# A second of seven block products made from halved blocks, with VectorE's order written out

## Chip, cores and metric

One core of one Trainium2 chip. The metric is the time on the device, in microseconds, of one execution of the whole program. Engines: TensorE (PE) multiplies; VectorE (DVE) and ScalarE (ACT) work elementwise; GpSimd (POOL) is nearly idle; SyncE (SP) issues most DMA transfers in the order of its queue.

## The reference

A decoder block on x of 1024 rows and 1024 columns, in float32: a pooling mixer beside windowed attention, merged by gates, and then an MLP with normalisation around it. The change concerns the MLP's second multiplication and what feeds it:

```python
D_MODEL = 1024; SEQ = 1024; D_FF = 4 * D_MODEL
...
    h2 = _rmsnorm(x, g_mlp_pre[l])
    ff = jnp.einsum('bsf,fd->bsd',
                    jnp.square(jax.nn.relu(jnp.einsum('bsd,df->bsf', h2, w_up[l]))), w_down[l])
    x = x + _rmsnorm(ff, g_mlp_post[l])
```

Below f is the squared relu (1024 x 4096), w_dn is w_down (4096 x 1024), and Down is f times w_dn with the closing normalisation.

## The kernel before

Every large matmul is made on operands split into a high and a low part: `split(hi, lo, src)` casts `src` to `hi` on ScalarE (L101) and subtracts to get `lo` on VectorE (L104). Each product then takes three matmuls, high by high, high by low, low by high (`PASSES`). The tiles of split parts are called `wh` for f and `ar` for w_dn; `raw` and `st` are staging tiles of unsplit data, `B` are resident tiles of w_dn's four blocks (B11, B12, B21, B22).

Down is computed as 2 x 2 blocks by a scheme with seven block products instead of eight. The sums of f that the scheme needs are made in the up stage (`store()`, called for pairs of row tiles) and kept in DRAM (`f_dram`, seven column blocks, `A_OF` tells which one a product reads). The sums and differences of w_dn's blocks are made in Down on VectorE (`differences`, `last_weights`, and the line in `operands` for product 5). `PRODUCTS = (1, 5, 2, 3, 6, 7, 4)` is the order of the products. Each has 8 steps over the contraction (`s_`), so Down has 56 steps, numbered j. In a plain step `down_mm` (L2075) makes 24 matmuls of 128x128 by 128x512 into four PSUM banks.

Product 6 is made by the same scheme once more, on blocks halved again: `quarters` prepares a step and `quarters_mm` (L2055) makes 42 matmuls with 256 columns in it, seven parts of six. Such a step needs four split operands: f1 (the block's own quarters), f2 (three sums of quarters of f, kept in DRAM in `spill`), w1 (three quarters of the weight block), w2 (four sums T of quarters of the weight block, L2009 to L2011). Three of the seven parts are added onto what product 1 left in `u` (`ONTO`, copied into the banks by ScalarE at L2050). `quarters_close` (L2061 to L2069) adds the seven parts up into `u` at the end.

While TensorE works on step j, the operands of step j + 2 are prepared (`AHEAD`). The scheduler of the language orders each engine's instructions, except inside `manual_schedule`, where the order of the code is kept: before, VectorE's order is given for the operands of products 6, 7 and 4, and the last step of product 6. An engine takes its instructions in that order and waits at each for what it needs. Tiles come from pools with a fixed number of buffers, and a new tile's first writer waits for the last reader of the buffer's old one. So f2 and w2 of a halved step s + 2 wait for the end of TensorE's step s, and w1 of step s + 1 waits for the sixth part of step s.

Names of weights: `wh<-raw` with 768 elements is f2's low part, `ar<-T` with 1024 is w2's, `ar<-B` with 512 and 256 is w1's (two pieces), `wh<-raw` with 1024 is f1's or that of a plain step's f.

Of the kernel before, what the change touches and what calls it, by code (L numbers as in the profile page):

```python
# [8 lines left out]
F32 = mybir.dt.float32  # L9
# [5 lines left out]
P = 128  # L15
# [35 lines left out]
def block_kernel(ctx: ExitStack, tc, xt, x, consts, vecs, sinks, b_qkv, g_post, g_mlp, g_mlp_post,  # L51
# [1565 lines left out]
    def up_close0(m, f):  # L1617
# [4 lines left out]
        def store():  # L1622
# [11 lines left out]
            if m // 2 % 2 == 0:  # L1634
                dve.tensor_tensor(s2[:, 256:], s2[:, :256], s2[:, 256:], ALU.subtract)
                s2_even.append(s2)
            else:
                a = s2_even.pop()
                e = g32([3, 256])
                dve.tensor_tensor(e[:, 1, :], s2[:, 256:], a[:, 256:], ALU.subtract)  # L1640
                dve.tensor_tensor(e[:, 0, :], e[:, 1, :], a[:, :256], ALU.add)
                dve.tensor_tensor(e[:, 2, :], s2[:, :256], e[:, 1, :], ALU.subtract)
                q.dma_start(e_dram(m // 4), e)
# [5 lines left out]
    stores, s2_even = [], []  # L1649

    def e_dram(s_):
        return spill[s_][:, :768].rearrange("p (a b) -> p a b", b=256)
# [9 lines left out]
    def up_square(m, f):  # L1662
        act.activation(f, f, AF.Square)
        f_odd[m] = f
        nc.scalar.dma_start(f_dram[m // 2][:, 2:4, :], f.rearrange("p (a b) -> p a b", b=512))
# [271 lines left out]
    def acc4(name):  # L1937
        return [dl.tile([P, 512], F32, tag="acc", name=nm(name), bufs=12) for _ in range(4)]
# [11 lines left out]

    def resident(name, s_):
        t = rp.tile([P, 2, 512], F32, tag="w", name=nm(name))
# [3 lines left out]
    def streamed(name, s_):  # L1956
        t = raw_tile()
        nc.sync.dma_start(t, w_block(name, s_))
        return t

    behind = []

    def operands(i, s_):
# [3 lines left out]
        else:  # L1967
            ft = stage([2, 512]) if (i, s_) == (1, 3) else raw_tile()
            nc.sync.dma_start(ft, f_block(A_OF[i], s_))
            if i == 1:  # L1970
# [3 lines left out]
                wt = res["B11", s_]  # L1974
            elif i == 5:
                resident("B12", s_)
                wt = res["B11", s_]
                dve.tensor_tensor(wt, res["B12", s_], wt, ALU.subtract)
            elif i == 2:
                wt = streamed("B21", s_)  # L1980
            elif i == 3:
                resident("B22", s_)
                wt = res["B22", s_]
            elif i == 6:
                wt = res["B11", s_]
            elif i == 7:
                wt = res["B12", s_]
            else:
                wt = res["B21", s_]
        if i == 6:  # L1990
            quarters(s_, ft, wt)
            return
# [348 lines left out]
```

## Time and profile before

| What | Value |
| --- | --- |
| median of 3 runs | 1090.21 us (1090.16 to 1090.69) |
| the profiled execution | 1091.0 us |
| its span, first to last instruction | 1089.2 us, granted clock 0.999 |
| Down, from product 1's first matmul to the end | from 779.30 us |
| order of products in it | 1, 5, 2, 3, 6, 7, 4 |
| VectorE busy in all | 849.2 us (78%) |
| ScalarE busy in all | 625.5 us (57%) |

A row of groups reads: line, engine, operation, out<-in by the program's names, shapes, count, then busy us in all, mean ns of one, idle time of the engine ahead of them with its releaser. A row of waits reads: engine and line, the releaser, then us in all, times, and the longest. A row of the chain reads: start, us, engine, line, count. A row of the timeline reads: start, us, engine, line, operation, count, and in brackets the idle time before. In a timeline several instructions of one kind in a row stand together, with their time from the first start to the last end.

### The profile page before, as it was taken

What the parts mean: (1) busy time and instruction counts of PE and PEld (TensorE: products, weight loads), DVE (VectorE), ACT (ScalarE), POOL (GpSimd) and SP (SyncE); (2) the same over time, 40 slices, a digit from 0 to 9 for tenths busy, and PEclk for the clock granted to TensorE, in tenths of its full rate; (3) what the DMA queues carried; (4) which work ended last, traced back from release to release, by engine and by line L of the source; (5) the groups of instructions that cost most, each with busy time, mean ns of one, the idle gap of its engine ahead of it and who ended that gap; (6) DMA issues with size and microseconds to landing.
All of it is one profiled execution on the core that took longest, in us unless ns stands there. A gap on an engine that the chain in (4) does not pass through costs nothing.

```text
span 1089.2 us, 14332 instructions
## 1 busy us (share of the span) xinstructions
PE 1079.7 (99%) x5211; PEld 903.5 (83%) x5211; DVE 849.2 (78%) x1194; ACT 625.5 (57%) x1029; POOL 86.2 (8%) x142
## 2 busy tenths in 40 slices
PE   9999999999999999999999999999999999999997
PEld 8888888888888888888888888888888888898885
DVE  6688888989897887889876766665657867579996
ACT  7567886456654257567665554555446535476543
POOL 0354411100100012100000000000000000000000
PEclk9999999999999999999999999999999999999999
DMA  9666889679965776832566534445597873379622
GB/s 333 201 174 175 214 251 350 184 233 315 268 213 171 223 191 137 288 117 77 185 227 227 205 143 174 160 150 216 177 391 272 299 265 118 101 234 318 218 78 78
DMA packets 100921, 227.36 MB, mean 209 GB/s; under 512 B 10481, under 2 KB 28017, under 8 KB 100849
## 3 DMA queue, kind: packets, MB, share of 16 engines
q1 hardware_dynamic: 84416, 189.46, 50.8%
q0 software_dynamic: 10528, 16.78, 8.8%
q10 hardware_dynamic: 5904, 20.19, 4.8%
q8 instruction: 41, 0.67, 0.3%
q14 instruction: 32, 0.25, 0.1%
HBM read 161.38 MB, written 63.97 MB: 207 GB/s over the span
## 4 chain that ended last, share of the span: by engine, by line
PE 75%; DVE 4%; ACT 1%; issue 1%; DMA 1%; ACTq 0%; DVEq 0%
PE mm L583 18%; PE at L583 15%; PE at L2075 12%; PE mm L2075 11%; PE mm L1523 5%; PE mm L494 3%; PE at L2055 2%; PE at L1523 2%; PE at L1251 2%; PE mm L2055 2%; PE mm L1251 1%; PE mm L496 1%; PE at L1569 1%; DMA st<-in_w_g_dram 1%; DVE xf L2121 0%
## 5 line engine op out<-in xcount | busy, mean ns | idle before, releaser
L2075 PE MATMUL at<-ar,wh 128*128 128x512 f32 x552 | 126.0, 389 | 0.2 <-DVE ar L104 0.2
L2075 PEld LDWEIGHTS at<-ar,wh 128*128 128x128 f32 x552 | 103.4, 188 | 22.1 <-DVE ar L104 0.6
L2075 PE MATMUL mm<-ar,wh 128*128 128x512 f32 x528 | 120.5, 389 | 0.0
L2075 PEld LDWEIGHTS mm<-ar,wh 128*128 128x128 f32 x528 | 99.1, 188 | 20.5
L101 ACT CAST wh<-raw 128x1024 fp32r<-128x1024 f32 (+1 forms) x58 | 59.2, 1023 | 86.2 <-PE at L2075 37.0
L104 DVE TENSOR_TENSOR wh<-st,wh 128x512 fp32r<-128x512 f32 (+1 forms) x103 | 74.4, 733 | 38.9 <-ACT wh L101 34.3
L104 DVE TENSOR_TENSOR wh<-raw,wh 128x1024 fp32r<-128x1024 f32 (+1 forms) x58 | 68.4, 1186 | 40.8 <-ACT wh L101 40.6
L583 PE MATMUL mm<-T,wx 128*128 128x512 f32 x375 | 90.3, 389 | 0.0
L583 PEld LDWEIGHTS mm<-T,wx 128*128 128x128 f32 x375 | 70.4, 188 | 14.6
L583 PE MATMUL mm<-gr,wh 128*128 128x512 f32 x321 | 77.2, 391 | 0.0
L101 ACT CAST wh<-st 128x512 fp32r<-128x512 f32 (+2 forms) x102 | 65.8, 654 | 19.2 <-PE at L583 4.6
L583 PEld LDWEIGHTS mm<-gr,wh 128*128 128x128 f32 x321 | 59.9, 188 | 12.2
L583 PE MATMUL mm<-T,wh 128*128 128x512 f32 x267 | 66.0, 389 | 0.0
L104 DVE TENSOR_TENSOR ar<-B,ar 128x1024 fp32r<-128x1024 f32 (+2 forms) x51 | 50.9, 1011 | 14.7 <-ACT ar L101 14.4
L583 PE MATMUL at<-gr,wh 128*128 128x512 f32 x243 | 59.0, 389 | 0.0
L583 PE MATMUL mm<-x,wh 128*128 128x512 f32 x240 | 58.9, 394 | 0.0
L583 PEld LDWEIGHTS mm<-T,wh 128*128 128x128 f32 x267 | 50.1, 188 | 10.4
L101 ACT CAST ar<-B 128x1024 fp32r<-128x1024 f32 (+2 forms) x51 | 44.1, 882 | 19.3 <-PE mm L2055 6.4
L583 PEld LDWEIGHTS at<-gr,wh 128*128 128x128 f32 x243 | 45.6, 188 | 9.5
L583 PEld LDWEIGHTS mm<-x,wh 128*128 128x128 f32 x240 | 44.2, 188 | 9.6 <-ACT f L692 0.2
L583 PE MATMUL at<-T,wx 128*128 128x512 f32 x213 | 52.0, 389 | 0.0
L583 PEld LDWEIGHTS at<-T,wx 128*128 128x128 f32 x213 | 40.0, 188 | 8.3
(529 smaller groups left out, 2264.5 us busy)
## 6 DMA issues: line engine op xcount, KB each, us to landing
raw<-f_dram SPq DMA_DIRECT2D x52, 512.0 KB, 4.7
B<-in_w_dn_dram SPq DMA_DIRECT2D x32, 512.0 KB, 6.5
f_dram<-g SPq DMA_DIRECT2D x28, 512.0 KB, 2.8
st<-in_w_up_dram SPq DMA_DIRECT2D x24, 512.0 KB, 4.5
g<-spill_dram SPq DMA_DIRECT2D x17, 512.0 KB, 5.7
f_dram<-g ACTq DMA_DIRECT2D x17, 512.0 KB, 2.9
st<-in_w_g_dram SPq DMA_DIRECT2D x16, 512.0 KB, 4.7
g<-in_w_up_dram SPq DMA_DIRECT2D x15, 512.0 KB, 4.8
```

Of the source, the lines that this page charges most:

```text
L101: act.copy(hi, src)
L104: return eng.tensor_tensor(lo, src, f32(hi), ALU.subtract)
L494: pe.matmul(bs[th], whi[:, k, :], rhs(k, hl, th), start=k == 0 and hl == 0, stop=False)
L496: pe.matmul(bs[th], wlo[:, k, :], rhs(k, 0, th), start=False, stop=k == nk - 1)
L583: pe.matmul(b, w[wh][:, kt, :], x_, start=not after and kt == 0 and j == 0, stop=kt == 3 and j == 2, skip_group_check=after)
L1251: pe.matmul(b, w[wh][:, kt, :], xo[xh][:, kt, :], start=not after and kt == 0 and j == 0, stop=kt == 1 and j == 2, skip_group_check=after)
L1523: pe.matmul(bs[t], Am[a][k][ah][:, t * P:(t + 1) * P], Wm[w][k][wh], start=not after and k == 0 and j == 0, stop=k == 3 and j == 2, skip_g ...
L1569: pe.transpose(b[:, i, :], hs[4 * th + i][:, k * P:(k + 1) * P], ident)
L2055: pe.matmul(part[q][:, t, :], o[fs][fh][:, fk, t * P:(t + 1) * P], o[ws][wh][:, wk, :], start=q not in ONTO and (s_, t, j) == (0, 0, 0), s ...
L2075: pe.matmul(bs[t], fo[fh][:, k2, t * P:(t + 1) * P], wo_[wh][:, k2, :], start=not after and s2 == 0 and k2 == 0 and j == 0, stop=(s2, k2) ...
```

## The change

Product 2 is made as product 6 is, by seven products of halved blocks, and comes right behind product 1; the order becomes 1, 2, 5, 3, 6, 7, 4. Product 2's close writes to a new tile `c4` (it becomes `c11`), product 6's to `u4` as before. In the up stage `store()` also makes the quartered sums of f's column block 2, and half of one block is stored later. All of Down's VectorE order is the order of the code now: per step j first `operands(j + 2)`, then what `extras(j)` lists. Resident tiles of w_dn are queued on SP behind the f load of the step (`later`). The pool of resident tiles, the accumulators and the tags of PSUM banks are counted anew.

```diff
@@ up stage, store() @@
             if m // 2 % 2 == 0:
                 dve.tensor_tensor(s2[:, 256:], s2[:, :256], s2[:, 256:], ALU.subtract)
-                s2_even.append(s2)
+                dve.tensor_tensor(g[:, 256:512], g[:, :256], g[:, 256:512], ALU.subtract)
+                q.dma_start(fd[:, 2, :], g[:, :512])
+                evens.extend((g[:, :512], s2))
             else:
-                a = s2_even.pop()
-                e = g32([3, 256])
...
-                q.dma_start(e_dram(m // 4), e)
+                for i, b in ((2, g[:, :512]), (6, s2)):
+                    a = evens.pop(0)
+                    e = g32([3, 256])
+                    dve.tensor_tensor(e[:, 1, :], b[:, 256:], a[:, 256:], ALU.subtract)
+                    dve.tensor_tensor(e[:, 0, :], e[:, 1, :], a[:, :256], ALU.add)
+                    dve.tensor_tensor(e[:, 2, :], b[:, :256], e[:, 1, :], ALU.subtract)
+                    q.dma_start(e_dram(i, m // 4), e)
...
     def up_square(m, f):
...
-        nc.scalar.dma_start(f_dram[m // 2][:, 2:4, :], f.rearrange("p (a b) -> p a b", b=512))
+        j = 2 if m // 2 % 2 else 3
+        nc.scalar.dma_start(f_dram[m // 2][:, j:4, :], f.rearrange("p (a b) -> p a b", b=512)[:, j - 2:, :])
@@ Down @@
+    def later(name, s_):
+        with tc.issue_after(behind[0].ins):
+            resident(name, s_)
...
-        if i == 6:
-            quarters(s_, ft, wt)
+        if i in HALVED:
+            quarters(i, s_, ft, wt)
...
-    def differences(s_):
-        b11, b12, b22 = (res[n, s_] for n in ("B11", "B12", "B22"))
-        dve.tensor_tensor(b11, b22, b11, ALU.subtract)
-        w = halved(b11)
-        dve.tensor_tensor(b12, b22, b12, ALU.subtract)
-        tt = res["T", s_] = rp.tile([P, 4, 256], F32, tag="w", name=nm("T"))
+    def first_sum(s_):
+        dve.tensor_tensor(res["B11", s_], res["B12", s_], res["B11", s_], ALU.subtract)
+
+    def next_sums(s_):
+        for n in ("B11", "B12"):
+            dve.tensor_tensor(res[n, s_], res["B22", s_], res[n, s_], ALU.subtract)
+
+    def last_sum(s_):
+        dve.tensor_tensor(res["B11", s_], res["B21", s_], res["B11", s_], ALU.subtract)
+
+    def quarter_sums(name, s_):
+        w = halved(res[name, s_])
+        tt = res["T", s_] = rp.tile([P, 4, 256], F32, tag="T", name=nm("T"), bufs=4)
         dve.tensor_tensor(tt[:, 0:2, :], w[:, 1::2, :], w[:, 0:2, :], ALU.subtract)
         dve.tensor_tensor(tt[:, 2, :], w[:, 3, :], tt[:, 0, :], ALU.subtract)
         dve.tensor_tensor(tt[:, 3, :], w[:, 2, :], tt[:, 2, :], ALU.subtract)
...
-    PRODUCTS = (1, 5, 2, 3, 6, 7, 4)
+    PRODUCTS = (1, 2, 5, 3, 6, 7, 4)
+    HALVED = (2, 6)
...
+    def extras(j):
+        def at(first):
+            return 0 <= j - first < NS
+        if at(3):
+            later("B21", j - 3)
+        if at(4):
+            quarter_sums("B21", j - 4)
+        if at(11):
+            later("B12", j - 11)
+        if at(12):
+            first_sum(j - 12)
+        if at(16):
+            square_x1(j - 16)
+        if at(18):
+            later("B22", j - 18)
+        if 17 <= j < 21:
+            fin_half(j - 17, 0, c11[j - 17])
+        if at(20):
+            next_sums(j - 20)
+        if at(26):
+            quarter_sums("B11", j - 26)
...
+    def down_step(j, i, s_):
+        last = s_ == NS - 1
+        if i in HALVED and last:
+            with tc.manual_schedule(engines=CORE):
+                quarters_mm(i, s_)
+                quarters_close(c4 if i == 2 else u4)
+        if j + AHEAD < len(steps):
+            operands(*steps[j + AHEAD])
+        if i in HALVED:
+            if not last:
+                quarters_mm(i, s_)
+            extras(j)
+            return
...
+    with tc.manual_schedule(engines={mybir.EngineType.DVE}):
+        for j in range(1, AHEAD):
+            operands(*steps[j])
+        for j, step in enumerate(steps):
+            down_step(j, *step)
```

Two places on VectorE show the order. The first is the run of instructions for a halved step. Before, in product 6 (f2's low part, w2's, w1's in two pieces, f1's, and then the next step's f2, w2, w1 and f1):

```order
L104 TENSOR_TENSOR wh_8494<-raw_8491,wh_8493 128x768
L104 TENSOR_TENSOR ar_8496<-T_8219,ar_8495 128x1024
L104 TENSOR_TENSOR ar_8502<-B_1091_7123,ar_8501 128x512
L104 TENSOR_TENSOR ar_8502<-B_1091_7123,ar_8501 128x256
L104 TENSOR_TENSOR wh_8504<-raw_8489,wh_8503 128x1024
L104 TENSOR_TENSOR wh_8561<-raw_8558,wh_8560 128x768
L104 TENSOR_TENSOR ar_8563<-T_8225,ar_8562 128x1024
```

The same run after, in product 2 (L2007 to L2009 are the sums T that a later step uses):

```order
L104 TENSOR_TENSOR wh_7451<-raw_7448,wh_7450 128x768
L104 TENSOR_TENSOR ar_7453<-T_7386,ar_7452 128x1024
L104 TENSOR_TENSOR ar_7459<-B_1123_7332,ar_7458 128x512
L104 TENSOR_TENSOR ar_7459<-B_1123_7332,ar_7458 128x256
L104 TENSOR_TENSOR wh_7461<-raw_7446,wh_7460 128x1024
L2007 TENSOR_TENSOR T_7522<-B_1147_7436 128x512
L2008 TENSOR_TENSOR T_7522<-B_1147_7436,T_7522 128x256
L2009 TENSOR_TENSOR T_7522<-B_1147_7436,T_7522 128x256
L104 TENSOR_TENSOR wh_7531<-raw_7528,wh_7530 128x768
L104 TENSOR_TENSOR ar_7533<-T_7438,ar_7532 128x1024
```

Between f1 of one step and f2 of the next now stand the three instructions that make T. The second place is the close of a halved product. Before, at the end of product 6 (the operands of product 7's first step, the close, the operands of its second step):

```order
L104 TENSOR_TENSOR wh_8760<-raw_8757,wh_8759 128x1024
L104 TENSOR_TENSOR ar_8762<-B_1117_7271,ar_8761 128x1024
L2062 TENSOR_TENSOR st_8854<-st_8854,at_8369 128x512
L2063 TENSOR_TENSOR st_8855<-st_8854,at_8368 128x512
L2065 TENSOR_TENSOR u_7026<-u_7026,at_8368 128x2x256
L2066 TENSOR_TENSOR st_8855<-st_8854,at_8371 128x512
L2068 TENSOR_TENSOR u_7026<-st_8855,mm_8372 128x2x256
L2068 TENSOR_TENSOR u_7026<-st_8854,mm_8374 128x2x256
L2068 TENSOR_TENSOR u_7026<-st_8855,mm_8376 128x2x256
L2069 TENSOR_TENSOR u_7026<-u_7026,st_8855 128x2x256
L104 TENSOR_TENSOR wh_8871<-raw_8868,wh_8870 128x1024
L104 TENSOR_TENSOR ar_8873<-B_1123_7308,ar_8872 128x1024
```

After, at the end of product 2 (L1995 is `first_sum`, L2057 to L2064 the close, and the operands are those of product 5):

```order
L104 TENSOR_TENSOR wh_7873<-raw_7870,wh_7872 128x1024
L104 TENSOR_TENSOR ar_7875<-B_1089_7142,ar_7874 128x1024
L1995 TENSOR_TENSOR B_1103_7218<-B_1225_7867,B_1103_7218 128x1024
L2057 TENSOR_TENSOR st_7969<-st_7969,mm_7469 128x512
L2058 TENSOR_TENSOR st_7970<-st_7969,mm_7468 128x512
L2060 TENSOR_TENSOR c_7083<-u_7082,mm_7468 128x2x256
L2061 TENSOR_TENSOR st_7970<-st_7969,mm_7471 128x512
L2063 TENSOR_TENSOR c_7083<-st_7970,at_7472 128x2x256
L2063 TENSOR_TENSOR c_7083<-st_7969,at_7474 128x2x256
L2063 TENSOR_TENSOR c_7083<-st_7970,at_7476 128x2x256
L2064 TENSOR_TENSOR c_7083<-c_7083,st_7970 128x2x256
L104 TENSOR_TENSOR wh_7984<-raw_7981,wh_7983 128x1024
```

The close stands between the same two pairs of operands; differences for product 5 (`first_sum`) now stand in the same queue, one right ahead of the close, and others behind each further pair of operands.

163 lines of the change are left out of this document (54 added, 109 removed).

## The prediction

> **What bounds the kernel now.** I read the page's busy times first, then TensorE's waits, the end of the chain of waits, busy time by stage for the seven Down products, and the groups and timelines around product 6, which is already made as seven halved products and so is the model for product 2.
>
> ```profile
> span 1089.2 us, 14332 instructions
> PE 1079.7 (99%) x5211; PEld 903.5 (83%) x5211; DVE 849.2 (78%) x1194; ACT 625.5 (57%) x1029; POOL 86.2 (8%) x142
> PE mm L200 <- PEq L2327: 0.8, 1, 0.8
> PE sc L182 <- ACT x L203: 0.6, 1, 0.6
> PE at L2075 <- DVE ar L104: 0.2, 1, 0.2
> PE at L583 <- DVE z L1168: 0.2, 1, 0.2
> 779.30 43.52 PE at L2075 x192
> 822.82 43.52 PE mm L2075 x192
> 866.34 43.52 PE at L2075 x192
> 909.86 43.52 PE mm L2075 x192
> 953.38 2.87 PE at L2055 x24
> ```
>
> TensorE is busy for 99% of the span, and all its waits together are 1.8 us: matmuls bound the kernel. A plain product is 192 matmuls in 43.52 us (226.7 ns each, 5.44 us for a step of 24), without a gap. Product 2 is the third of them (866.34).
>
> ```profile
> 993.69 6.58 PE L2075 MATMUL at<-ar,wh 128*128 128x512 f32 x28
> 1000.47 7.78 PE L2075 MATMUL at<-ar,wh 128*128 128x512 f32 x33 [0.21 <-DVE ar L104]
> 779.30:822.80 43.50, 43.50 (x194) 36.03 (x193) 26.93 (x27) 19.37 (x22) 0.00 (x0) 1.00 0.87 317
> 953.40:993.70 40.30, 40.30 (x337) 40.19 (x337) 32.36 (x38) 31.44 (x44) 0.00 (x0) 1.00 0.79 255
> 958.26:988.50 30.24, 30.24 (x253) 30.13 (x252) 25.20 (x30) 22.17 (x31) 0.00 (x0) 1.00 0.83 269
> ```
>
> The last three rows are stretches: length, then busy time of TensorE, weight loads, VectorE, ScalarE and GpSimd, granted clock, DMA share, GB/s. Product 6 (halved) runs from 953.38 to 993.69: 336 matmuls of 256 columns in 40.31 us, 120 ns each, 5.04 us for a step of 42. The third stretch is six of its steps: VectorE is busy 25.20/6 = 4.20 of every 5.04 us. So 0.84 us per step is free on VectorE, and that is the number on which this change turns.
>
> **The change, part by part.**
>
> *Fewer matmul columns.* Product 2 goes from 43.52 to 40.32 us of TensorE: -3.2. [...]
>
> *VectorE's work per step.* A halved step needs the 4.20 us above, and its weight sums T on top. In before these sums lie ahead of product 6, where there is room; after, T for step s of product 2 is made four iterations of the step loop ahead of its use, so four of eight fall into product 2, and a fifth between the operands of its first and second steps. VectorE's order is now given, so nothing overtakes them.
>
> ```profile
> L2009 DVE TENSOR_TENSOR T<-B 128x512 f32<-128x512 f32 x8 | 5.5, 690 | 0.2
> L2011 DVE TENSOR_TENSOR T<-B,T 128x256 f32<-128x256 f32 x8 | 3.4, 424 | 0.2
> L2010 DVE TENSOR_TENSOR T<-B,T 128x256 f32<-128x256 f32 x8 | 3.4, 422 | 0.2
> 958.50 1.03 DVE L104 TENSOR_TENSOR ar<-B,ar 128x512 fp32r<-128x512 f32 x2 [1.96 <-ACT ar L101]
> 959.44 2.09 DVE L104 TENSOR_TENSOR wh<-raw,wh 128x1024 fp32r<-128x1024 f32 x2
> ACT ar L101 <- PE mm L2055: 6.4, 7, 1.3
> ```
>
> The sums cost 0.690 + 0.424 + 0.422 = 1.54 us, so a round with them is 4.20 + 1.54 = 5.74 us, 0.70 longer than TensorE's step. A lead cannot pay for that: the last row shows that ScalarE's first weight cast of the next step waits for TensorE to leave the tile, in each of seven steps, so VectorE is never more than about a step ahead.
>
> The start: in before VectorE begins the second step's first-half weights at 958.50, 5.12 us after product 6 began, behind ScalarE's copies. Into product 2 ScalarE has two more copies to make there, against a cast that can start earlier:
>
> ```profile
> 952.53 1.07 ACT L2251 COPY c<-mm 128x512 f32<-128x512 f32 x2
> 953.49 0.85 ACT L101 CAST wh<-raw 128x768 fp32r<-128x768 f32 x1
> 957.85 0.92 ACT L101 CAST ar<-B 128x512 fp32r<-128x512 f32 x2
> ```
>
> 5.12 + 1.07 - 0.3 (my estimate of the earlier cast) = 5.9 us after product 1's end, which is the clock's zero below.
>
> *The lateness at product 2's end.* VectorE, back to back:
>
> ```profile
> 993.15 0.68 DVE L2062 TENSOR_TENSOR st<-st,at 128x512 f32<-128x512 f32 x1
> ...
> 998.06 1.22 DVE L104 TENSOR_TENSOR wh<-raw,wh 128x1024 fp32r<-128x1024 f32 x1
> 999.20 1.22 DVE L104 TENSOR_TENSOR ar<-B,ar 128x1024 fp32r<-128x1024 f32 x1
> 1000.34 1.22 DVE L104 TENSOR_TENSOR wh<-raw,wh 128x1024 fp32r<-128x1024 f32 x1
> L1978 DVE TENSOR_TENSOR B<-B,B 128x1024 f32<-128x1024 f32 x8 | 9.8, 1220 | 0.9 <-DMA B<-in_w_dn_dram 0.9
> ```
>
> The close of a halved product takes 998.06 - 993.15 = 4.91 us, each 128x1024 operation 1.14 us start to start, a plain step's pair 2.28 us, and a difference for product 5 (the L1978 row, same form) 1.14 too. Five rounds with T: 5.9 + 28.7 = 34.6. One with a difference instead: 4.20 + 1.14, to 39.9. The last halved step's second half 2.1, to 42.0; difference 1.14; operands of product 5's first step 2.28, to 45.4; difference 1.14, to 46.6; close 4.91, to 51.5; operands of product 5's second step 2.36 (until the last one ends), to 53.8. TensorE then has 20 of that step's 24 matmuls left (four need only high parts; the 28 before the wait at 1000.47 are 24 + 4 of the same kind): 20 x 0.2267 = 4.53, to 58.4. Without waits these ten steps take 40.32 + 10.88 = 51.2. So 7.2 us late; 6.4 if VectorE starts at 5.12 as in product 6. As a floor I take 5.3: the list from 5.9 to 53.8 is 47.9 us long, and 4% off every operation (my estimate of how far such rows can be off) is 1.9.
>
> *Product 6.* Its T sums move too: five of eight lie in product 3, three between its own steps. Start at 5.12, three rounds of 5.74, to 22.3; TensorE has 35 of the fifth step's 42 matmuls left, 4.2, to 26.5 against 25.2 without waits: +1.3. The later rounds of 4.20 fit, so it stays at that. Low end 0, if high-part matmuls pulled ahead cover it.
>
> *Edits that I cost at nothing.* The up stage's extra halves: per pair one or three 128x256 subtractions and 384 KB of spill on every second pair. Four pairs with 0.42 and four with 1.26 us (L2011's row, 0.424) are 6.7 us of VectorE over some 330 us, in which TensorE waits for VectorE 0.2 us in all (the z row above). If the cover is gone it is at the entry to Down:
>
> ```profile
> 796.99 1.23 DVE L104 TENSOR_TENSOR wh<-raw,wh 128x1024 fp32r<-128x1024 f32 x1 [4.21 <-ACT wh L101]
> 798.67 1.23 DVE L104 TENSOR_TENSOR ar<-B,ar 128x1024 fp32r<-128x1024 f32 x1 [0.46 <-ACT ar L101]
> 806.91 1.22 DVE L104 TENSOR_TENSOR ar<-B,ar 128x1024 fp32r<-128x1024 f32 x1 [0.16 <-ACT ar L101]
> 809.57 1.23 DVE L104 TENSOR_TENSOR ar<-B,ar 128x1024 fp32r<-128x1024 f32 x1
> 790.00:795.00 5.00, 5.00 (x23) 4.13 (x22) 1.23 (x1) 1.05 (x1) 0.00 (x0) 1.00 1.03 397
> ```
>
> The fifth step's operands are done at 799.9; TensorE wants them at 779.30 + 21.76 = 801.1. 1.2 us are spare, and the DMA engines are full there (share 1.03 at 397 GB/s): 384 KB more are 1.0 us at that rate. I take 0, with +1 as the other end. The resident loads of B21 now stand in SP's queue behind each step's f, ahead of the next one: at 397 GB/s each pushes the later ones by 1.3 us, one ahead of the seventh step and two ahead of the eighth, which have 811.9 - 808.1 = 3.8 and 817.4 - 810.8 = 6.6 us to spare. In product 2 a step moves 512 + 384 + 512 KB in 5.04 us, 286 GB/s, below the 317 of product 1's row. Cost 0. Plain differences, squares of x1 and gains ride on VectorE's 16.6 idle us of a plain product (43.50 - 26.93). Accumulator buffers, tags and banks cost nothing by themselves: close reads a bank before TensorE's order comes to it, as in 6 to 7 now. Products 7 and 4 keep their content.
>
> **Sum.** -3.2 + 7.2 + 1.3 = +5.3 us. The profiled run took 1091.0 us (span 1089.2), 0.8 above the median of 1090.21; so 1096.3 for such a run, and 1095.5 by the median. A change of under 0.2% (2.2 us) could not be told from none here.
>
> **Rivals.**
> 1. *VectorE's lead absorbs the sums: faster, 1087.0.* Mechanism: high-part matmuls pulled ahead, together with the free 0.84 us, cover 1.54. For it: TensorE has no wait in product 6 today. Against it: 0.70 us per round in five rounds plus a close that lies ahead of operands. It decides where a round of VectorE with T is at most 5.04 us; the rows give 5.74. If the close's lateness alone stayed at 6 to 7's size (44.20 against 43.50 now, 0.7), the time is 1087.7. Chance 0.10.
>
> ```profile
> 993.70:1037.90 44.20, 43.99 (x195) 36.01 (x194) 42.89 (x57) 23.40 (x31) 0.00 (x0) 1.00 0.73 252
> ```
>
> 2. *The floor: stalls about as large as the saving.* 5.3 late at product 2, nothing in product 6: -3.2 + 5.3 = +2.1, 1092.3, or within 0.2%. Chance 0.13.
> 3. *Transfers late as well.* A halved step's spill load waits for a staging tile that VectorE's now late operands free, and ScalarE then waits for the spill:
>
> ```profile
> ACT wh L101 <- DMA raw<-spill_dram: 1.5, 2, 0.8
> ```
>
> 0.75 us each time; in five steps +3.7, over the sum: 1099.2. Against it: today only two of eight steps wait, and off the path. Chance 0.12.
> 4. *The forecast*, 1093 to 1098: 0.65.
>
> Slower holds 0.65 + 0.12 and a little of the floor, 0.78; same 0.12; faster 0.10. The range leaves out rival 1 and the upper part of rival 3: 1091 to 1099.
>
> **What would show it.** Right: in the changed kernel TensorE waits at the quartered matmuls for VectorE's ar and wh, some 0.7 us per step from product 2's third step on; one wait of about 3 us at product 5's second step, behind the close; product 2 lasting about 44.9 us (42.0 and its last 24 matmuls) in spite of 40.3 of work; VectorE busy for 98% from 6 us into product 2 to the close; about 1.3 us of waits in product 6's first half and none in its second. Wrong: no waits in product 2, or a VectorE that idles on ScalarE there (then a round is shorter than my sum, or the lead longer); waits on DMA at product 1's fifth step; product 6 longer than 42 us.

## The result, and the profile after

The changed kernel takes 1100.34 us (median of four, 1099.06 to 1101.33) against 1090.45 us (1090.16 to 1090.69) beside it: ratio 1.009, 95% interval 1.0073 to 1.0108. It is 9.9 us slower. The forecast was slower by 5.3, with a range that ended at 1099. The profiled execution is the shortest of the four, 1099.06 us; its span is 8.1 us longer than the one profiled before.

Busy times from the page, and TensorE's waits, of the changed kernel:

```profile
span 1097.3 us, 14810 instructions
PE 1080.7 (98%) x5355; PEld 907.8 (83%) x5355; DVE 888.0 (81%) x1282; ACT 638.6 (58%) x1053; POOL 86.4 (8%) x142
PE at L2070 <- DVE ar L104: 2.6, 2, 2.1
PE mm L2050 <- DVE ar L104: 2.0, 6, 0.6
PE at L2050 <- DVE ar L104: 0.3, 1, 0.3
```

TensorE now waits for VectorE at the halved matmuls (L2050), where it did not wait before, and at plain ones (L2070): 2.1 us at product 5's second step and 0.5 us at product 1's fifth. The waits listed are not all of the lateness: single matmuls that start late one by one are not in them. So I measured each stage from its first matmul to the next stage's first, in every profile (us; "ideal after" is the number of the changed kernel's matmuls at 226.7 and 120 ns):

| Stage | ideal after | before | changed | e9 | e13 |
| --- | --- | --- | --- | --- | --- |
| up to product 1 | | 779.1 | 779.0 | 779.5 | 779.6 |
| product 1 | 43.5 | 43.5 | 44.6 | 44.6 | 43.5 |
| product 2 (halved after) | 40.3 | 43.5 | 44.2 | 41.5 | 41.5 |
| products 5 and 3 | 87.0 | 87.0 | 89.6 | 88.05 | 88.06 |
| product 6 | 40.3 | 40.5 | 41.4 | 40.3 | 40.3 |
| products 7 and 4, to the last matmul | 87.0 | 87.9 | 88.2 | 87.3 | 87.3 |
| from the last matmul to the end (tail) | | 7.66 | 10.22 | 7.28 | 7.29 |

(Before, products 1, 5, 2 and 3 together took 174.1, four times 43.5. e9 and e13 are two of the experiments below.) The 8.1 us between the two profiled executions are thus: -3.2 for the halved matmuls, +6.4 late in product 2 and behind its close, +1.1 in product 1, +1.0 in product 6, +0.3 in 7 and 4, +2.6 in the tail, -0.1 ahead of Down. The medians lie 9.9 apart: the profiled execution before is 0.6 above its median, the changed one 1.3 below its own. Where these other 1.8 us lie no profile shows.

The three places where it happens, in the timelines. First VectorE at the head of product 2, then its close; product 2 begins at 823.65:

```profile
825.44 0.96 DVE L104 TENSOR_TENSOR wh<-raw,wh 128x768 fp32r<-128x768 f32 x1 [1.74 <-ACT wh L101]
829.44 1.03 DVE L104 TENSOR_TENSOR ar<-B,ar 128x512 fp32r<-128x512 f32 x2 [1.90 <-ACT ar L101]
...
835.04 1.02 DVE L104 TENSOR_TENSOR ar<-B,ar 128x512 fp32r<-128x512 f32 x2
...
840.64 1.02 DVE L104 TENSOR_TENSOR ar<-B,ar 128x512 fp32r<-128x512 f32 x2
...
869.27 0.68 DVE L2057 TENSOR_TENSOR st<-st,mm 128x512 f32<-128x512 f32 x1
...
875.31 1.22 DVE L104 TENSOR_TENSOR ar<-B,ar 128x1024 fp32r<-128x1024 f32 x1
```

A round with a sum T is 5.60 us (829.44, 835.04, 840.64), back to back, 0.56 more than TensorE's step of 5.04. From 6 us into product 2 to the close VectorE is busy for 99% of the time. The close begins 45.6 us after product 2's start and the second step's operands are ready at 52.9. But ahead of the first round VectorE stands idle for 1.74 and 1.90 us, with the sums T queued behind the waiting instructions.

Second, the entry to Down, SyncE's queue and TensorE:

```profile
794.51 0.37 SPq L1975 DMA_DIRECT2D raw<-f_dram  x1
802.22 4.15 PE L2070 MATMUL at<-ar,wh 128*128 128x512 f32 x17 [0.52 <-DVE ar L104]
```

The f load of product 1's fifth step goes out at 794.51. The chain that ends at this step's matmuls shows what it waited for, the store of the added sums:

```profile
787.78 6.65 DMA spill_dram<-g
794.45 0.03 SPq L1975
```

In the kernel before the load went out at 787.28:

```profile
787.28 0.37 SPq L1969 DMA_DIRECT2D raw<-f_dram  x1
```

Third, the sums that close the last four tiles on VectorE, and TensorE's last matmuls:

```profile
1077.73 0.69 DVE L2261 TENSOR_TENSOR u<-u,at 128x512 f32<-128x512 f32 x1 [1.54 <-PE at L2070]
1081.77 0.68 DVE L2261 TENSOR_TENSOR u<-u,mm 128x512 f32<-128x512 f32 x1
1085.73 0.68 DVE L2261 TENSOR_TENSOR u<-u,mm 128x512 f32<-128x512 f32 x1
1089.70 0.68 DVE L2134 TENSOR_TENSOR u<-u,mm 128x512 f32<-128x512 f32 x1
1086.18 0.88 PE L2131 MATMUL at<-hold,hold 128*128 128x256 f32 x6
```

One tile takes VectorE about 4.0 us, and here the tiles follow each other; the last tile's sum starts 3.5 us after the last six matmuls have started. In the kernel before the second tile begins inside the first, 1.95 us after it, and the last sum starts only 0.7 us after the last six matmuls. The first sum there starts 11.4 us ahead of the end of the last matmul, in the changed kernel 9.3 us:

```profile
1070.18 0.69 DVE L2262 TENSOR_TENSOR u<-u,mm 128x512 f32<-128x512 f32 x1 [1.51 <-PE mm L2075]
1072.13 0.67 DVE L2262 TENSOR_TENSOR u<-u,mm 128x512 f32<-128x512 f32 x1
1077.39 0.68 DVE L2262 TENSOR_TENSOR u<-u,mm 128x512 f32<-128x512 f32 x1
1081.36 0.68 DVE L2139 TENSOR_TENSOR u<-u,mm 128x512 f32<-128x512 f32 x1
```

### The profile page after: what moved, and what is told of

The parts are those of the page before. It is cut to its first block, busy times and chain, and to the rows that moved or that the text cites. A ratio compares the mean times of both kernels' runs of the same rounds, so it can differ in the third digit from the quotient of the medians.

```text
span 1097.3 us, 14810 instructions
## 1 busy us (share of the span) xinstructions
PE 1080.7 (98%) x5355; PEld 907.8 (83%) x5355; DVE 888.0 (81%) x1282; ACT 638.6 (58%) x1053; POOL 86.4 (8%) x142
## 4 chain that ended last, share of the span: by engine, by line
PE 88%; DVE 7%; ACT 2%; DMA 2%; issue 1%; DVEq 0%; SPq 0%; ACTq 0%
PE mm L583 25%; PE at L583 18%; PE mm L2070 9%; PE at L2070 8%; PE mm L1523 5%; PE mm L494 3%; PE mm L191 2%; PE sc L182 2%; PE mm L182 2%; PE at L1523 2%; PE at L1251 2%; PE at L2050 2%; DVE ar L104 2%; DVE wh L104 2%; PE mm L1251 1%; PE mm L2050 1%
## 5 line engine op out<-in xcount | busy, mean ns | idle before, releaser
L2070 PE MATMUL at<-ar,wh 128*128 128x512 f32 x444 | 111.6, 390 | 2.6 <-DVE ar L104 2.6
L2070 PE MATMUL mm<-ar,wh 128*128 128x512 f32 x444 | 111.4, 389 | 0.2 <-DVE ar L104 0.2
L101 ACT CAST wh<-raw 128x1024 fp32r<-128x1024 f32 (+1 forms) x66 | 65.8, 999 | 70.7 <-PE mm L2070 23.2
L2070 PEld LDWEIGHTS at<-ar,wh 128*128 128x128 f32 x444 | 83.0, 188 | 21.2 <-DVE ar L104 3.8
L2070 PEld LDWEIGHTS mm<-ar,wh 128*128 128x128 f32 x444 | 83.2, 188 | 17.9 <-DVE ar L104 0.7
L104 DVE TENSOR_TENSOR wh<-raw,wh 128x1024 fp32r<-128x1024 f32 (+1 forms) x66 | 76.0, 1156 | 22.1 <-ACT wh L101 22.0
L104 DVE TENSOR_TENSOR ar<-B,ar 128x1024 fp32r<-128x1024 f32 (+1 forms) x67 | 59.1, 901 | 12.5 <-ACT ar L101 12.1
L101 ACT CAST ar<-B 128x1024 fp32r<-128x1024 f32 (+1 forms) x67 | 51.3, 792 | 20.6 <-PE mm L2050 6.7
L583 PEld LDWEIGHTS mm<-T,wh 128*128 128x128 f32 x267 | 50.0, 188 | 10.9 <-ACT g L612 0.6
L583 PEld LDWEIGHTS at<-gr,wh 128*128 128x128 f32 x243 | 45.6, 188 | 9.5
L583 PEld LDWEIGHTS mm<-x,wh 128*128 128x128 f32 x240 | 44.2, 188 | 9.6 <-ACT f L692 0.2
L2050 PE MATMUL mm<-ar,wh 128*128 128x256 f32 x336 | 49.3, 285 | 2.0 <-DVE ar L104 2.0
```

What stands on the lines that cost most here:

```text
L101: act.copy(hi, src)
L104: return eng.tensor_tensor(lo, src, f32(hi), ALU.subtract)
L583: pe.matmul(b, w[wh][:, kt, :], x_, start=not after and kt == 0 and j == 0, stop=kt == 3 and j == 2, skip_group_check=after)
L2050: pe.matmul(part[q][:, t, :], o[fs][fh][:, fk, t * P:(t + 1) * P], o[ws][wh][:, wk, :], start=q not in ONTO and (s_, t, j) == (0, 0, 0), s ...
L2070: pe.matmul(bs[t], fo[fh][:, k2, t * P:(t + 1) * P], wo_[wh][:, k2, :], start=not after and s2 == 0 and k2 == 0 and j == 0, stop=(s2, k2) ...
```

## The experiments

Ratios are against the kernel before, on the same chip, with their 95% intervals. The medians of different experiments come from different chips (the kernel before took 1090.45 to 1091.11 us beside them), so small differences between them are rough; where two profiles are compared, the stages are used.

**e1, the tail's order free.** Edit (the last step outside the given order):

```diff
-        for j, step in enumerate(steps):
+        for j, step in enumerate(steps[:-1]):
             down_step(j, *step)
+    down_step(len(steps) - 1, *steps[-1])
```

> The changed kernel with one edit: Down's last step (the closing of the last four tiles) stands outside the given order, so VectorE's order there is the scheduler's again. Theory A (the tail of the changed kernel is 2.8 us longer, behind the last matmul, because VectorE takes one tile's chain after another): 2 to 3 us below the changed kernel's 1100.3, so 1097.3 to 1098.3, and VectorE's last sums start within 1 us of the last matmul's end. Rival C (the tail is longer because TensorE finishes the tiles in another order): no change, 1100.3.

1100.19 us, ratio 1.008 (1.0065 to 1.0094). The executions spread from 1098.0 to 1102.4, too wide to tell the theory from the rival; e6 is the same edit once more.

**e2, T left out in four steps.** Edit: `quarter_sums("B21", j - 4)` only for j < 8, and steps 4 to 7 of product 2 take the T of steps 0 to 3.

> The changed kernel with the weight sums T of product 2's last four steps left out (those steps use the sums of the first four; the output is not the reference's). Theory A: the 0.3 to 0.6 us that TensorE waits at each step of product 2 disappear, the close then starts at about 42 us after product 1's end instead of 46.6, and product 5's second step is 2.7 us late instead of about 6 to 7: 3.5 us below the changed kernel, about 1096.8. Rival B (halved steps cannot be fed at product 2's place anyway, by ScalarE or by transfers): waits stay, 1100.3.

1098.49 us, ratio 1.0064 (1.0052 to 1.0076), 1.7 below the changed kernel's later median of 1100.23 and not 3.5. The waits inside product 2 went as expected (it took 41.5 us instead of 44.2). But products 5 and 3 took 91.2 instead of 89.6: the wait behind the close stayed at 2.11 us, and behind it the clock was halved (granted clock 0.50 from 876 to 878; see e5). Without T, VectorE is bound by TensorE, which must leave w1's tile: its wait of 1.01 us for ScalarE's cast of w1, before 855.18, lies behind that cast's own wait of 1.11 us for TensorE. And from there the last operands, two differences, the close and the next operands make 14 us in a row. So T is one part of the lateness and the list around the close another, in this order.

**e3, T on GpSimd.** Edit: the three `dve.tensor_tensor` in `quarter_sums` become `pool.tensor_tensor`.

> The changed kernel with all weight sums T (products 2 and 6) made on GpSimd instead of VectorE; nothing else changed. GpSimd's 128x128 sums take 0.5 to 0.7 us in the trace of before, so one set of T (a 128x512 and two 128x256) should take 4 to 5.6 us on it. Theory A: where it stays below a step's 5.04 us, product 2's waits go as if T was left out, and product 6's too: 4.5 us below the changed kernel, 1095.8. Rival B: unchanged, 1100.3. Rival D (GpSimd is too slow or takes time from VectorE): waits for T grow by 0.5 us per step or VectorE's operations get longer, 1102 or more.

1106.58 us, ratio 1.0142 (1.0128 to 1.0155): rival D. One set of T alone on GpSimd, in product 1, and the means of VectorE's operations in product 2 (groups by shape) with it:

```profile
807.23 1.28 POOL L2007 TENSOR_TENSOR T<-B 128x512 f32<-128x512 f32 x1 [323.44 <-DMA B<-in_w_dn_dram]
808.59 0.74 POOL L2008 TENSOR_TENSOR T<-B,T 128x256 f32<-128x256 f32 x1
809.41 0.74 POOL L2009 TENSOR_TENSOR T<-B,T 128x256 f32<-128x256 f32 x1
```

```profile
L104 DVE TENSOR_TENSOR wh<-raw,wh 128x1024 fp32r<-128x1024 f32 x9 | 13.7, 1519 | 0.0
L104 DVE TENSOR_TENSOR ar<-T,ar 128x1024 fp32r<-128x1024 f32 x7 | 9.6, 1370 | 0.0
L104 DVE TENSOR_TENSOR ar<-B,ar 128x512 fp32r<-128x512 f32 x7 | 5.9, 836 | 3.3 <-ACT ar L101 3.3
```

Alone a set takes 2.8 us, faster than I had put it. But VectorE's 1024-wide operation takes 1519 ns instead of 1218, and its 512-wide one 836 instead of 686. In product 2 VectorE is busy for 42.9 us instead of 40.2, though it makes 15 sums fewer; product 2 takes 46.2 us (44.2 in the changed kernel) and product 6 44.3 (41.4). The work given away came back as longer operations of VectorE. Single operations show it as well: w2's low part took 1.76 us at 834.55, where a sum of GpSimd ran beside it to 835.23, and 1.21 at 841.35, between two sums of GpSimd. Why they take longer side by side this trace does not show.

**e4, the tail's given order alone, in the kernel before.** Edit: the closing of the last four tiles wrapped in `tc.manual_schedule(engines={mybir.EngineType.DVE})`.

> The kernel before with one part of the change alone: VectorE's order given in the closing of the last four tiles. Theory A: 2 to 3 us above before, 1092.5 to 1093.5, with the last sums starting 2 us or more behind the last matmul. Rival C: 1090.4, as before.

1092.0 us against 1091.1, ratio 1.0007 (0.9998 to 1.0016): by the times not clear of no change. By the profile the time from the last matmul to the end is 8.47 instead of 7.66, and the four sums stand 3.97 to 4.03 us apart, as in the changed kernel. The mechanism is there and costs 0.8, not 2 to 3, and here the first sum starts 11.4 us ahead of the end of the last matmul, in the changed kernel 9.3; that the smaller cost comes from this lead is a reading of the two profiles.

**e5, the changed kernel again**, beside e6 to e8.

> The changed kernel itself, as the base on this chip for the three beside it. Theory: 1099 to 1101, and the executions differ by whether TensorE's clock is halved for one 3.4 us window behind the 2.1 us wait at product 5's second step (1.7 us): executions with a mean granted clock of 0.996 or less take 1 to 2 us longer than those with 0.997 or more. Rival (the executions differ for another reason, transfers say): no relation between clock and time.

1100.23 us (1099.98 to 1100.97). Its profiled execution is one with a clock of 0.995, and shows where. Stretches of it (the column after GpSimd is the granted clock), and TensorE's timeline:

```profile
866.00:875.00 9.00, 8.71 (x47) 7.06 (x45) 8.97 (x13) 4.95 (x8) 0.00 (x0) 1.00 0.84 291
875.00:878.00 3.00, 1.17 (x4) 0.98 (x5) 3.00 (x4) 2.25 (x4) 0.00 (x0) 0.92 0.04 6
878.00:880.00 2.00, 2.00 (x6) 1.52 (x6) 2.00 (x2) 1.97 (x5) 0.00 (x0) 0.50 0.86 240
880.00:886.00 6.00, 6.00 (x26) 4.90 (x25) 6.00 (x7) 5.58 (x10) 0.00 (x0) 0.92 1.05 404
```

```profile
876.84 0.72 PE L2070 MATMUL at<-ar,wh 128*128 128x512 f32 x2 [2.12 <-DVE ar L104]
877.40 2.67 PE L2070 MATMUL mm<-ar,wh 128*128 128x512 f32 x6
```

The same matmuls in the first profile of the changed kernel:

```profile
876.58 0.73 PE L2070 MATMUL at<-ar,wh 128*128 128x512 f32 x2 [2.10 <-DVE ar L104]
877.16 1.53 PE L2070 MATMUL mm<-ar,wh 128*128 128x512 f32 x6
```

The clock is missing 0.08 x 3 + 0.50 x 2 + 0.08 x 6 = 1.7 us, that is 3.4 us at half rate, right behind the 2.1 us wait; six matmuls take 2.67 us where they took 1.53. Products 5 and 3 last 91.2 instead of 89.6. The wait of 2.10 us in the first profile was not followed by a halved clock (granted clock 1.00 from 876 to 888 there). Over the eight executions of this kernel the six with a mean clock of 0.997 took 1100.0 on average and the two below 1101.2, which fits the theory, on two executions. The wait itself, 2.1 us, is shorter than the 3.4 us at half rate behind it; why an equal wait was followed by a halved clock in one execution and not in another, no run shows.

**e6, e1's edit again.**

> As e1 (VectorE's order left to the scheduler in the closing of the last four tiles), once more for a profile and beside the changed kernel on the same chip. Theory A (as corrected by e4, where the given order alone cost 0.9 us in the kernel before): 0.8 to 1.8 us below the changed kernel; the rest of the 2.6 us of tail comes from tiles that TensorE finishes later. Rival C: no change.

1098.91 us, ratio 1.0074 (1.0061 to 1.0086), 1.3 below e5. In its profile the time from the last matmul to the end is 8.16 instead of 10.22. Two of the last sums on VectorE:

```profile
1079.29 0.69 DVE L2261 TENSOR_TENSOR u<-u,at 128x512 f32<-128x512 f32 x1 [1.52 <-PE at L2070]
1080.90 0.68 DVE L2261 TENSOR_TENSOR u<-u,mm 128x512 f32<-128x512 f32 x1
```

1.6 us apart instead of 4.0. So the order given in the last step costs 2.1 us in the tail of this kernel by the profiles, and 1.3 by the medians.

**e7, the spill stores behind f's.** Edit: in `store()` the quartered sums are stored after the three stores of f.

> The changed kernel, with the stores of the quartered sums queued behind the stores of f in each pair, so that the f loads of Down need not wait for them. Theory (the fifth step of product 1 is 1.0 us late because its f load stands at the head of SP's queue until the last spill store has landed): the load is issued near 790 instead of 794.5, TensorE's wait of 0.5 at product 1's fifth step goes, and the kernel is 1.0 us faster than the changed one. Rival (the DMA engines are full there, and the transfers take as long in any order): no change.

1101.5 us, ratio 1.0098 (1.0082 to 1.0113), no gain: the load still went out at 795.22. The rival holds as far as the order of the stores goes; e12 takes the wait away in another way.

**e8, differences one step later.** Edit: `if at(13): first_sum(j - 13)` for `if at(12): first_sum(j - 12)`.

> The changed kernel, with each difference for product 5 made one step of the loop later, so that one less (1.14 us) stands ahead of product 2's close. Theory A (VectorE's list between product 2's start and the operands of product 5's second step sets the end): those operands are ready 1.1 us sooner, 1.1 us below the changed kernel, and more (to 2.8) where the shorter wait no longer halves the clock. Rival (ScalarE or the banks set it): no change.

1100.47 us, ratio 1.0086 (1.0072 to 1.0099): no gain. The second step's operands were ready 52.5 us after product 2's start instead of 52.9, so 0.4 sooner and not 1.1: with one operation less ahead of the close VectorE waited 0.41 us for ScalarE's cast, which had waited 0.74 us for TensorE. The bound next to VectorE's list lies only that far below it.

**e9, all of Down's given order undone.** Edit:

```diff
-    with tc.manual_schedule(engines={mybir.EngineType.DVE}):
+    with nullcontext():
         for j in range(1, AHEAD):
```

> The changed kernel with the given VectorE order undone for all of Down (the scheduler decides, except for the last step of products 2 and 6 and the last tile). Theory A (VectorE's amount of work in product 2 is the cause, not its order; the order costs only in the tail): product 2 as long as in the changed kernel within 1 us, the tail 2 us shorter, so 1098 to 1099 as in e6. Rival (the given order itself causes the waits in product 2): 1095 or less.

1090.47 us against 1090.93, ratio 0.9996 (0.9987 to 1.0005). The rival was right and theory A fell: the same work, in the scheduler's order, takes as long as the kernel before. VectorE at the head of product 2 in e9, which begins at 824.11, and TensorE at product 5's second step:

```profile
823.64 0.68 DVE L2007 TENSOR_TENSOR T<-B 128x512 f32<-128x512 f32 x1
824.36 0.43 DVE L2008 TENSOR_TENSOR T<-B,T 128x256 f32<-128x256 f32 x1
824.82 0.43 DVE L2009 TENSOR_TENSOR T<-B,T 128x256 f32<-128x256 f32 x1
825.18 1.22 DVE L104 TENSOR_TENSOR ar<-T,ar 128x1024 fp32r<-128x1024 f32 x1
826.32 0.95 DVE L104 TENSOR_TENSOR wh<-raw,wh 128x768 fp32r<-128x768 f32 x1
827.19 0.69 DVE L2007 TENSOR_TENSOR T<-B 128x512 f32<-128x512 f32 x1
...
828.87 1.23 DVE L104 TENSOR_TENSOR wh<-raw,wh 128x1024 fp32r<-128x1024 f32 x1
830.01 1.02 DVE L104 TENSOR_TENSOR ar<-B,ar 128x512 fp32r<-128x512 f32 x2
```

```profile
872.85 0.73 PE L2070 MATMUL at<-ar,wh 128*128 128x512 f32 x2 [0.69 <-DVE ar L104]
```

Where VectorE stood idle for 3.6 us in the changed kernel, sums T and f1's low part run now; w1 starts at 5.9 us (5.8 in the changed kernel), but with that work behind it: five sets of T are done by then, three in the changed kernel. The stretch from 823.6 to 867.8 in the changed kernel and in e9:

```profile
823.60:867.80 44.20, 42.15 (x337) 40.70 (x337) 40.22 (x55) 31.94 (x45) 0.00 (x0) 1.00 0.80 262
```

```profile
823.60:867.80 44.20, 43.57 (x349) 42.67 (x349) 43.36 (x59) 34.33 (x48) 0.00 (x0) 1.00 0.90 302
```

VectorE is busy 43.4 of 44.2 us instead of 40.2. Behind the close the wait is 0.69 instead of 2.10. There, too, the order shows: the f operand that product 5's second step needs stands between two sums of the close, where the changed kernel made it behind the close:

```profile
866.25 1.21 DVE L104 TENSOR_TENSOR wh<-raw,wh 128x1024 fp32r<-128x1024 f32 x1
```

Product 2 and its close are 2.2 late instead of 6.4 (table above), and product 6 and the tail have no loss. The tail is not mended by closer sums: they stand 4.0 us apart in e9 as well. What differs is that the first sum starts 12.3 us ahead of the end of the last matmul and not 9.3, and that VectorE has the last operands (`hold`) of products 7 and 4 ready 16.2 us ahead of that end instead of 10.9. The last of these operands and the first two sums in e9, then that operand in the changed kernel:

```profile
1063.90 1.22 DVE L104 TENSOR_TENSOR hold<-B,hold 128x1024 fp32r<-128x1024 f32 x1
1069.00 0.69 DVE L2261 TENSOR_TENSOR u<-u,at 128x512 f32<-128x512 f32 x1 [3.88 <-PE at L2070]
1073.02 0.68 DVE L2261 TENSOR_TENSOR u<-u,mm 128x512 f32<-128x512 f32 x1
```

```profile
1074.97 1.22 DVE L104 TENSOR_TENSOR hold<-B,hold 128x1024 fp32r<-128x1024 f32 x1
```

One limit of e9: with VectorE's order undone the scheduler moved instructions of other engines too. ScalarE, for one, copies the first of product 1's banks at 823.57 and the others later, where the changed kernel copies all three together at 826.27. So the run shows what the whole schedule is worth; that the work queued behind VectorE's waiting instructions is the part that counts is read from the timelines.

**e10, the up stage's part alone, in the kernel before.** The new `store()` and `up_square` in the kernel before. Product 2, plain there, reads block 2 of f as it is stored for halves, so its result is not the product; the work is that of a plain product.

> The kernel before with one part of the change alone: the up stage makes and stores the quartered sums of block 2 (nothing reads them) and stores half of that block later. Theory A (up stage hidden, the entry to Down pays for the added 384 KB): TensorE has one wait of 0.2 to 0.5 at product 1's fifth step, and the kernel takes 0.3 to 1.1 us more than before. Rival (VectorE's extra subtractions delay the up stage): waits of TensorE at the up stage's lines, 2 us or more.

1092.66 us, ratio 1.0018 (1.0009 to 1.0026): slower by 1.7, more than the 0.3 to 1.1 expected. TensorE waits 0.53 us at product 1's fifth step and nowhere in the up stage, but the last matmul is 1.2 us further from the start of Down than before. So by the profile most of the entry's cost comes with the up stage's part.

**e11, product 2 plain in the changed kernel.** `HALVED = (6,)`, banks as before, no T for it; product 2 reads block 2 as in e10.

> The changed kernel with the halving of product 2 undone: product 2 is a plain product in the same place, without its T sums; the order of the products, VectorE's given order, the queues and the up stage's stores are those of the changed kernel. Theory A (halving gives 3.2 us and costs 6.4; the rest of the change costs 1.1 at the entry, 1.0 in product 6 and 2.6 in the tail): 3 to 3.5 us below the changed kernel's executions without a halved clock, 1096 to 1097. Rival (halving is about neutral, and the order of products and queues costs the 9 us): 1099 to 1100.

1097.62 us, ratio 1.007 (1.0057 to 1.0082). With the order given, halving itself costs 1100.23 - 1097.62 = 2.6 us, a little under the 3 to 3.5 of theory A; the rest of the change costs 6.7.

**e12, the entry and the tail mended.** e1's edit and

```diff
-            ft = stage([2, 512]) if (i, s_) == (1, 3) else raw_tile()
+            ft = stage([2, 512]) if (i, s_) in ((1, 3), (1, 4)) else raw_tile()
```

> The changed kernel with two repairs: VectorE's order free in the closing of the last four tiles (e6), and the f load of product 1's fifth step into a tile of the staging pool that is free early, so that it need not wait for the spill store. Theory: the load is issued before 790, TensorE's wait of 0.5 at that step goes (-1.0), the tail is 2 us shorter: 3 us below the changed kernel, 1097.3. Rival (the DMA engines are full until 820 in any case): only the 2 us of the tail, and the wait moves to the sixth or seventh step.

1097.68 us, ratio 1.0061 (1.0049 to 1.0074). This is near the theory's 1097.3. Product 1 takes 43.5 us again, without a wait: what the load waited for was its tile's memory, which a store of the up stage was still reading (from 787.78 to 794.43 in the chain above, with the load issued at 794.51). All five executions have a clock of 0.996, and in the profiled one the matmuls slow down behind the close: the six behind the wait of 2.09 us take 2.76 us, in e5 2.67.

**e13, order free and the entry mended.** e9 and e12's second edit.

> The changed kernel with VectorE's order free (e9) and the f load of product 1's fifth step into a free staging tile (e12's second edit). Theory (e9's account against before: -3.2 halving, +1.1 entry, +2.2 lateness around product 2's close, the rest as before): the entry's 1.1 go, 1089.3, faster than before by 0.15%. Rival (product 2's lateness takes up what the entry gives back, since VectorE is busy without a gap there): 1090.4, as e9.

1088.65 us (1088.31 to 1089.4) against 1090.62, ratio 0.9983 (0.9974 to 0.9991): faster than both kernels, as expected. In the table only the entry (product 1) differs from e9.

**e14, order given only from product 5 on.**

> The changed kernel with VectorE's order free for the first two products and given from product 5 on. Theory E (the given order costs 4.2 us in product 2 and its close, 1.1 in product 6, 2 to 3 in the tail, and the halved clock goes with the shorter wait): product 2 and its close 2.2 us late instead of 6.4, 1095 to 1096. Rival (the order costs mainly behind product 2): 1099 or more.

1095.02 us, ratio 1.0045 (1.0033 to 1.0058). Theory E: product 2 takes 41.3 us, products 5 and 3 88.05, as with the order free; product 6 (41.5) and the tail (10.2) are those of the changed kernel. Of the some 9.8 us between the changed kernel and e9, about half comes from the order in products 1 and 2 and about half from the order behind them: 5.2 and 4.6 by the medians, 4.6 and 5.3 by the ratios, 4.4 and 5.0 by the stages of the profiles.

**e15, T between w2 and w1, order given.** `quarter_sums("B21", s_ + 2)` is called in `quarters` behind w2.

> The changed kernel, its order still given, with each sum T of product 2 standing between w2 and w1 of the same operands instead of behind f1, so that one of them falls into the 1.9 us in which VectorE waits for ScalarE at the start of product 2. Theory E (what the given order costs there is idle time of VectorE with work queued behind it): one round with T less in the chain, product 5's second step ready 1.5 us sooner, about 1098.7. Theory A (the amount of work alone): no change, 1100.2.

1100.26 us, ratio 1.0082 (1.0067 to 1.0097): no change in the median. The operands of product 5's second step are ready 52.1 us after product 2's start instead of 52.9, and product 2 is 0.8 shorter (43.35), half of what theory E wanted; the 2.10 us wait remained, and in this profile the matmuls behind it run at the pace of e5's halved clock (six in 2.72 us), which takes the gain back. It neither bears out theory E nor excludes it; e14 does the former.

**e16, a fifth buffer for T**, on top of e13.

> As e13, with five buffers for T instead of four, so that the scheduler may make one sum earlier. Theory (VectorE is busy without a gap from the start of product 2 to the close, and every sum moved ahead of it takes 1.5 us off the lateness): 0.5 to 1.5 us below e13, 1088 to 1088.8. Rival (the loads of B21 arrive too late to use it): as e13.

1088.68 us, ratio 0.9981 (0.9972 to 0.999): as e13. The profile shows product 2 in 40.8 instead of 41.5 us, but no gain in time can be told.

**e17, the kernel before with its order free.** Its `given` always returns `nullcontext()`.

> The kernel before with its own given order (operands and sums of products 6, 7 and 4 on VectorE) left to the scheduler. Theory (in e13 product 6, product 7 and the tail together are 1.2 us shorter than in the kernel before, and that is the order): 0.6 to 1.2 us below before, about 1089.7. Rival (the given order of the kernel before costs nothing; the gain in e13 is from elsewhere): as before, 1090.6.

1090.21 us, ratio 0.9991 (0.9982 to 1.0): 0.6 below before, at the edge of what can be told. So some 0.6 of e13's 2.0 may come from freeing the order that the kernel before had already.

**e18, e13 with product 2 plain.** Product 2 reads block 2 as in e10.

> e13 with the halving of product 2 undone (order free, entry mended; product 2 plain in the same place). Theory (halving gives 3.2 and is 1.15 late in product 2 and 1.0 behind its close): 1.0 us above e13, 1089.7. Rival (with the order free the halving gives nothing): as e13, 1088.7.

1090.58 us, ratio 0.9996 (0.9987 to 1.0005). e13 is below it by 1.9 us by the medians, 1.4 by the ratios and 1.2 by the stages of the two profiles, and the intervals of the two ratios just overlap. So with VectorE's order free, halving product 2 is worth some 1.2 to 1.9 of its 3.2 us.

## Why the prediction was wrong, step by step

The way was right and the size was not: 9.9 us slower and not 5.3. In the profiled executions (8.1 us) the two terms of the sum came out 1.1 us smaller than forecast (7.4 for 8.5), and the step that failed was to put the rest at nothing: "Edits that I cost at nothing" and "Products 7 and 4 keep their content" hold at 0 what measured +1.1 at the entry to Down, +2.6 in the tail and +0.3 in products 7 and 4. One step of the mechanism failed as well, "A lead cannot pay for that", and there the size came near by luck.

*Saving.* The matmuls' own time is 3.2 us less, as forecast: product 6, without a wait in e9 and e13, takes 40.3. Product 2 itself came to 40.8 at best (e16), 2.7 less than plain.

*Lateness in product 2.* Forecast 7.2, measured 6.4. The round was 5.60 instead of 5.74, the close at 45.6 instead of 46.6, the second step's operands at 52.9 instead of 53.8. VectorE's list was summed rightly; that it had to stand so was wrong. I wrote that a lead cannot pay for the sums, since VectorE is never more than a step ahead. That holds for w1, whose tile TensorE must leave (ScalarE's casts of it waited 4.7 us for TensorE in product 2, in six steps); it does not hold for T, which has four buffers. I took the 5.9 us at the head of product 2 as the time when VectorE's work may start, while VectorE could have made two sets of sums in it. e9 and e14 show the size: with the order free there, the same operations are 2.2 late. So what I priced as amount of work was for two thirds (4.2 of 6.4) the order in which the work stood, as far as the other engines' changed order in e9 and e14 has no part in it.

*Product 6.* Forecast 1.3, measured 1.0, and none in e9: it goes with the order. e14 places it in the order given from product 5 on.

*The entry.* Costed at 0, with +1 as the other end; it was +1.1, and the sign that the forecast named for being wrong, a late load at product 1's fifth step, came. The step that failed is the price of the added spill stores: I counted their bytes against spare time, and not that the f load at the head of SyncE's queue waits for a store to leave a tile's memory (794.51 instead of 787.28). e12 shows it: with a tile of its own for the load, product 1 takes 43.5 again.

*The tail.* Costed at nothing, by "Products 7 and 4 keep their content". The content stayed, the order did not. In e9 the 2.6 us are gone, and in e14, with the order given from product 5 on, they are there: they go with the given order. The profiles show two ways. Freeing the last step alone lets the tiles overlap and takes 2.1 us away (e6). Freeing all of it leaves the tiles one after another, but the last operands are ready earlier and the first sum starts 12.3 us ahead of the end of the last matmul and not 9.3 (e9); in e6 and e12 it stays at 9.3.

*The up stage.* My count of its added subtractions was too low: `store()` runs for 16 pairs, so 8 with 0.42 us and 8 with 1.26 are 13.4 us and not 6.7. Nothing came of it; Down starts at 779.0 us, against 779.1 before.

*The clock.* Not in the forecast. It adds 1.6 us where a halved clock follows the 2.1 us wait (91.2 instead of 89.6 for products 5 and 3, in the profiles of e2, e5, e12 and e15).

*The rivals.* Rival 1 had the outcome that e9 and e13 come near to, a lead of VectorE that absorbs the sums, but by another mechanism (matmuls of high parts pulled ahead); it was given 0.10, since the sums were taken to stand where the order put them. Rival 3 (late transfers in product 2) appeared only as one wait of ScalarE for `spill` of 0.9 us. The signs named for the forecast came: waits at L2050 for ar, one wait behind the close (2.1 for the 3 forecast), product 2 at 44.2 for 44.9, VectorE busy for 99%. Of the signs of being wrong two came besides: VectorE idle on ScalarE, at the head of product 2 (1.74 and 1.90 us), and the late load at product 1's fifth step.

## What to carry to other kernels

In these runs a written order turned waits of its engine into idle time (VectorE's 1.74 and 1.90 us at the head of product 2), with work queued behind them that the scheduler's order did in that time (e9): so before pricing such an order by the sum of its operations, look at each instruction that waits and ask what could run there, and count the parts of the program that the order newly covers, the tail too. The same work took 1100.2 us in the written order and 1090.5 in the scheduler's. And where a load gets a new tile, what it waits for may be the last reader of the memory, not the data: here a store that ended at 794.43, with the load issued at 794.51 (e12).

## What the runs showed of the hardware

A wait of TensorE of 2.1 us, shorter than the 3.4 us at half rate that the granted clock shows behind it in e2 and e5, was followed by slower matmuls in four profiles (six in 2.29, 2.67, 2.76 and 2.72 us in e2, e5, e12 and e15); behind an equal wait in the first profile of the changed kernel six took 1.53 us. And sums moved from VectorE to GpSimd, otherwise idle in Down, went with slower operations of VectorE: 2.8 us for a set alone, VectorE's 1218 ns operation at 1519 on the mean, and a kernel of 1106.58 us instead of 1100.34.
